# High and low weight tiles as eight separate buffers, the high ones shifted by up to 128 bytes, and four raw buffers in place of five

## The chip, the cores and the metric

The kernel runs on one core of one Trainium2 chip. The metric is the device time of one execution in microseconds (us). Times agree between executions to about 0.1%: the two timed runs of the kernel before gave 1609.97 and 1611.32 us.

## What is computed

The reference is a decoder trunk of two layers over 256 tokens of width 2,048. Each layer normalises x, multiplies it by one wide input projection, sends the columns through a sparse-attention group and a state-space (SSD) group, normalises both results, joins them and multiplies by one output projection, whose result is added to x:

```python
def hybrid_layer(x, ...):
    h = rmsnorm(x, norm_w)
    proj = jnp.einsum("bsd,dp->bsp", h, w_in)          # 2048 -> 11856 columns
    (q, kc, vc, ks, vs, kw, vw, gate, z_attn, xbc, dt, z_ssm) = split_columns(proj)
    ...                                                # attention with three branches, conv, SSD
    mixed = jnp.concatenate([y_attn, y_ssm], axis=-1)  # 4096 wide
    return x + jnp.einsum("bsm,md->bsd", mixed, w_out)
```

All weights arrive in float32. The two projections of the two layers are nearly all of the weight bytes.

## The kernel before

**Weights as high and low parts.** A float32 product is put together from products in a shorter format (F32R). Each weight piece is split in two: `hi` is the weight rounded to F32R, `lo` is the weight less `hi`. The activations are split in the same way. A product is then activation-high times weight-high, activation-low times weight-high, and activation-high times weight-low.

**Slots.** The weights are cut into 250 pieces per layer, 500 in all (`NS` = 250, `DEPTH` = 2). A piece is one tile of 128 partitions by 1,024 float32, 512 KB, and the work on it is called a slot. 186 pieces per layer belong to the input projection (93 column tiles of 128 columns, each in two halves of the 2,048 inputs) and 64 to the output projection.

- In a slot of the input projection (L950 to L968) the weights are the stationary operand and the activations `src[k]` stream: 8 matmuls of `wh[:, k]` with 512 columns (high and low activations side by side) and 8 of `wl[:, k]` with 256 columns, in pairs: two high, two low. In layer 0 the streamed tiles are called `h`, in layer 1 `s`; each is 128 by 512 float32, 2,048 bytes per partition.
- In a slot of the output projection (`block`, L977 to L987) it is the other way: the mixed activations are stationary and the weights stream, 512 columns each. A slot has 12 matmuls, 8 that stream `wh` and 4 that stream `wl`.

**The pipeline of a weight piece.** SP issues the transfer of piece `d` from HBM into a raw tile `wr` (`pump_dma`, L147 to L152). ScalarE copies the raw tile into `wh` (L160, through the helper at L122). VectorE subtracts `wh` from the raw tile into `wl` (L166, through the helper at L125). TensorE reads `wh` and `wl`.

- Each of `wr`, `wh` and `wl` is a tag of the tile pool with a number of buffers used in turn: `NR` = 5 raw, `NH` = 4 high, `NL` = 4 low. A buffer is 4,096 bytes per partition, and the buffers of one tag lie one behind the other. A tile that takes a buffer again waits until the readers of the tile before it in this buffer are done.
- `split(i)` (L154 to L167) is called in slot `i`. It emits the high copy up to piece `i + LH` and the low one up to piece `i + LL` (both 2 ahead), and after each low one it calls `pump_dma`, which emits the transfers up to `state["lo"] + NR`. So the transfer that is emitted behind the low copy of piece `j` is the one of piece `j + 5`. It takes the raw buffer of piece `j`, and waits for that low copy.
- The instructions stand in each engine's queue in the order in which the program emits them; nothing reorders them there.

**Start.** Before the first slot the program issues by hand the first piece (three parts on ScalarE's queue), and on SP's queue the input x in five parts, pieces 1 to 4 between them (`pump_one`, L179), and then the parameters `prm` and the constants `cst` (L202, L203).

**Other work.** Between slots the program runs generators (`sides`) for convolution, SSD, attention and norms, whose instructions are placed by waiting counts written out by hand (`WAITS`). The tile `KT{g}` (L268), which holds the attention keys, has rows of 272 float32: its four parts `kt[:, b, t]` start 1,088 bytes apart.

Of the kernel before, what the change touches and what calls it, by code (L numbers as in the profile page):

```python
# [12 lines left out]
F32R = mybir.dt.float32r  # L13
# [74 lines left out]
def body(ctx: ExitStack, tc: tile.TileContext, wst, w1, xin, xtk, pos, w2, par, con, fin, y):  # L88
# [1 line left out]
    ACT, DVE, PE, POOL = nc.scalar, nc.vector, nc.tensor, nc.gpsimd  # L90
    RS, RA = 5, 1
    FIRST = ((0, 256), (256, 512), (512, 1024))
    NR, NH, NL, LH, LL = 5, 4, 4, 2, 2

    pp = ctx.enter_context(tc.tile_pool(name="pp", bufs=1))
    qq = ctx.enter_context(tc.tile_pool(name="qq", bufs=1, space=bass.MemoryType.PSUM))
# [5 lines left out]
    def sb(shape, tag, dt=F32, bufs=1):  # L102
        cnt[0] += 1
        return pp.tile(shape, dt, tag=tag, name=f"{tag}_{cnt[0]}", bufs=bufs)
# [11 lines left out]
    def act(out, in_, f=AF.Copy, **kw):  # L116
        if f in (AF.Ln, AF.Exp) and table[0] != AF.Exp:
            ACT.preload_act_table_set("natural_log_exp_and_others")
            table[0] = AF.Exp
        elif f in (AF.Silu, AF.Sin):  # L120
            table[0] = f
        ACT.activation(out, in_, f, **kw)  # L122
# [10 lines left out]
    def lo(out, full, hi):  # L133
        tt(out, full, f(hi), OP.subtract)
# [9 lines left out]
    raw, hi_t, lo_t = {}, {}, {}  # L144
    state = {"dma": 0, "hi": 0, "lo": 0}

    def pump_dma():  # L147
        while state["dma"] < min(state["lo"] + NR, DEPTH * NS):
            d = state["dma"]
            raw[d] = sb([128, 1024], "wr", bufs=NR)  # L150
            nc.sync.dma_start(raw[d], wst[d])
            state["dma"] += 1  # L152

    def split(i, part=1024):  # L154
        while state["hi"] < min(i + LH + 1, DEPTH * NS):
            j = state["hi"]
            state["hi"] += 1
            hi_t[j] = sb([128, 1024], "wh", F32R, bufs=NH)
            for c in range(0, 1024, part):
                act(hi_t[j][:, c:c + part], raw[j][:, c:c + part])  # L160
        while state["lo"] < min(i + LL + 1, DEPTH * NS):
            j = state["lo"]
            state["lo"] += 1
            lo_t[j] = sb([128, 1024], "wl", F32R, bufs=NL)
            for c in range(0, 1024, part):
                lo(lo_t[j][:, c:c + part], raw[j][:, c:c + part], hi_t[j][:, c:c + part])  # L166
            pump_dma()  # L167
# [11 lines left out]
    def pump_one():  # L179
        d = state["dma"]  # L180
        raw[d] = sb([128, 1024], "wr", bufs=NR)
        nc.sync.dma_start(raw[d], wst[d])
        state["dma"] += 1

    def load_x(a, b):
        c = NK + SEQ * a if a else 0
        nc.sync.dma_start(xw[:, c:NK + SEQ * b], xin[:, c:NK + SEQ * b])
# [10 lines left out]
    load_x(8, 12)  # L198
    pump_one()
    load_x(12, 16)  # L200
    pump_one()
    nc.sync.dma_start(prm, par[0])  # L202
    nc.sync.dma_start(cst, con)  # L203
    pump_dma()

    ident = cst[:, C_ID:C_ID + 128]
# [166 lines left out]
            scaled(attn[:, k], nw0[:, k:k + 1], h[k])  # L373

    state["hi"] = state["lo"] = 1
    hi_t[0] = sb([128, 1024], "wh", F32R, bufs=NH)
    lo_t[0] = sb([128, 1024], "wl", F32R, bufs=NL)
    for j, (a, b) in enumerate(FIRST):
        make_h((0, 1, 2)[j], (1, 2, 4)[j])
        act(hi_t[0][:, a:b], raw[0][:, a:b])  # L380
        lo(lo_t[0][:, a:b], raw[0][:, a:b], hi_t[0][:, a:b])
    make_h(4, 8)
    split(1 - LH)
    nc.gpsimd.dma_start(posi, bass.AP(tensor=pos.tensor, offset=pos.offset, ap=[[0, 128], [1, SEQ]]))

# [19 lines left out]
    for L in range(DEPTH):  # L405
# [524 lines left out]
        for it in ITEMS:  # L930
            if it[0] == "w":
                kv, j = it[1], it[2]
# [19 lines left out]
            if it[0] == "p":  # L952
# [3 lines left out]
                wh = hi_t[i].rearrange("p (k c) -> p k c", k=8)  # L956
                wl = lo_t[i].rearrange("p (k c) -> p k c", k=8)
                n = 2 if L or slot else 1
                for a in range(0, 8, n):
# [4 lines left out]
                    if L == 0 and slot == 0:  # L964
                        for _ in range(WARM[a]):
                            mm(pz, wz[:, 0:128], wz, True, True)
                flush()
                split(i)  # L968
            else:
                cb, kp, half = it[1:]  # L970
# [53 lines left out]
                if last4:  # L1024
                    if kp == 4:
                        split(i + 1)
                        for kq in range(4, 8):
                            block(kq, 0)
                            if kq == 4:
                                split(i + 1)  # L1030
                        add(0)
                        out_norm(0)
                    block(kp, 1)
                    if kp == 7:
                        add(1)
                        out_norm(1)
                else:
                    block(kp, 0)
                    flush()
                    if kp == 7:  # L1040
                        add(0)
                    block(kp, 1)
                    split(i)
                    if kp == 7:
                        add(1)
                        if half and L + 1 < DEPTH:
                            sides.append(turn())
# [136 lines left out]
```

## Time and profile before

| | us |
|---|---|
| median of the two timed runs | 1610.64 |
| the profiled execution, its own time | 1612.35 |
| span of the profiled execution, first to last instruction | 1610.6 |
| TensorE (PE) busy | 1582.5 |
| VectorE (DVE) busy | 1219.2 |
| ScalarE (ACT) busy | 1056.3 |
| GpSimd (POOL) busy | 383.9 |

The profiled execution took 1.7 us more than the median of the runs, and its span is that median to 0.1 us. How to read the profile: "busy" is the time in which an engine had an instruction under way. Matmuls are pipelined, so their single durations overlap and the spacing of their starts is what one of them costs. PEld is the load of the stationary operand, which runs beside the matmuls. The chain of work is followed back from the last instruction, at each step to what released it.

### The profile page before, as it was taken

Reading aid. Unit: us, or ns where it says so; the run is one execution under the profiler, and the core shown is the slowest. Engines: PE = TensorE matmul, PEld = TensorE weight load, DVE = VectorE, ACT = ScalarE, POOL = GpSimd, SP = SyncE. Lnnn points to the kernel's source line nnn. Section 1 sums busy time; section 2 is a strip of 40 time slices with the busy share of each in tenths; the row PEclk is TensorE's granted clock in tenths of the full one; section 3 lists DMA queues with packets and bytes.
Section 4 is the critical chain, followed back from the end, with each engine's and each line's share of the span. In section 5 each row is a group of like instructions: output and inputs, shape, how many; then the busy total and the mean of one; then the engine's idle time right before and its main releaser. Section 6 shows DMA issues by size and latency. Waiting matters only on the chain.

```text
span 1610.6 us, 24881 instructions
## 1 busy us (share of the span) xinstructions
PE 1582.5 (98%) x9042; PEld 1353.0 (84%) x9042; DVE 1219.2 (76%) x2113; ACT 1056.3 (66%) x1918; POOL 383.9 (24%) x314
## 2 busy tenths in 40 slices
PE   8999999999899999999999999999998999999997
PEld 7888888878788888888888888888787888888876
DVE  6888988887688786674578888888867878766654
ACT  6587777754687787544456777777447778865443
POOL 1233433431123231100012333333301323210010
PEclk9999999999999999999999999999999999999999
DMA  7575566677444444565646666666863454455653
GB/s 267 187 253 189 191 205 209 206 248 256 130 157 134 156 151 153 195 192 166 207 158 197 201 206 192 190 200 222 273 224 121 142 158 145 157 169 171 235 177 110
DMA packets 101994, 301.98 MB, mean 188 GB/s; under 512 B 9952, under 2 KB 26912, under 8 KB 101744
## 3 DMA queue, kind: packets, MB, share of 16 engines
q1 hardware_dynamic: 101024, 297.99, 56.4%
q0 software_dynamic: 416, 1.88, 0.4%
q8 instruction: 71, 1.16, 0.3%
q10 hardware_dynamic: 432, 0.52, 0.1%
q14 instruction: 51, 0.42, 0.1%
HBM read 298.20 MB, written 2.16 MB: 186 GB/s over the span
## 4 chain that ended last, share of the span: by engine, by line
PE 93%; DVE 2%; ACT 2%; DMA 1%; issue 1%; POOL 0%; ACTq 0%; SPq 0%; DVEq 0%; POOLq 0%
PE ppj L137 77%; PE po L137 7%; PE pb L137 6%; DVE wl L125 1%; ACT wh L122 1%; PE pt L137 1%; DMA wr<-wst 1%; PE pt L523 0%; PE pt L766 0%; PE po L773 0%; PE pt L767 0%; DMA V<-w 0%; DVE xT L125 0%; ACT A L122 0%; DVE A L128 0%
## 5 line engine op out<-in xcount | busy, mean ns | idle before, releaser
L125 DVE TENSOR_TENSOR wl<-wr,wh 128x1024 fp32r<-128x1024 f32 (+1 forms) x502 | 642.6, 1285 | 218.4 <-ACT wh L122 217.5
L122 ACT ACTIVATE wh<-wr 128x1024 fp32r<-128x1024 f32 (+1 forms) x502 | 517.8, 1048 | 85.6 <-PE ppj L137 46.2
L137 PE MATMUL ppj<-h,wh 128*128 128x512 f32 x1456 | 464.6, 400 | 3.1 <-DVE h L128 3.1
L137 PE MATMUL ppj<-s,wh 128*128 128x512 f32 x1456 | 462.7, 399 | 0.0
L137 PEld LDWEIGHTS ppj<-h,wl 128*128 128x128 f32 x1456 | 274.9, 189 | 65.1
L137 PEld LDWEIGHTS ppj<-s,wl 128*128 128x128 f32 x1456 | 274.4, 188 | 65.1
L137 PE MATMUL ppj<-h,wl 128*128 128x256 f32 x1456 | 288.3, 279 | 0.0
L137 PE MATMUL ppj<-s,wl 128*128 128x256 f32 x1456 | 287.3, 279 | 0.0
L340 POOL TENSOR_TENSOR uu<-uu,rr 128x256 f32<-128x256 f32 x120 | 147.7, 1232 | 525.3 <-DVE uu L125 524.0
L137 PEld LDWEIGHTS ppj<-h,wh 128*128 128x128 f32 x1456 | 223.4, 190 | 9.5 <-issue 3.3
L137 PEld LDWEIGHTS ppj<-s,wh 128*128 128x128 f32 x1456 | 222.8, 189 | 5.0 <-issue 2.7
L122 ACT ACTIVATE ev<-ppj 128x256 f32<-128x256 f32 x182 | 68.7, 378 | 210.7 <-PE ppj L137 193.7
L137 PE MATMUL ppj<-wh,h 128*128 128x512 f32 x384 | 120.4, 391 | 0.0
L137 PE MATMUL ppj<-wh,s 128*128 128x512 f32 x384 | 120.1, 391 | 0.0
L340 POOL TENSOR_TENSOR za<-za,rr 128x256 f32<-128x256 f32 x34 | 39.6, 1165 | 274.6 <-DVE za L125 239.2
L137 PEld LDWEIGHTS ppj<-wh,h 128*128 128x128 f32 x384 | 72.1, 188 | 15.6 <-DVE xT L125 0.7
L137 PEld LDWEIGHTS ppj<-wh,s 128*128 128x128 f32 x384 | 72.1, 188 | 15.5 <-DVE xT L125 0.7
L125 DVE TENSOR_TENSOR uu<-ppj,ev 128x256 f32<-128x256 f32 x116 | 48.7, 420 | 47.1 <-ACT ev L122 46.9
L122 ACT ACTIVATE A<-A,nm 128x128 f32<-128x128 f32 (+2 forms) x192 | 75.4, 394 | 7.8 <-DVE nm L716 7.6
L137 PE MATMUL ppj<-wl,s 128*128 128x512 f32 x192 | 74.9, 390 | 0.8 <-DVE wl L125 0.8
L137 PE MATMUL ppj<-wl,h 128*128 128x512 f32 x192 | 74.8, 389 | 0.0
L128 DVE SCALAR_TENSOR_TENSOR att<-uu,par,att 128x255 f32<-128x255 f32 (+2 forms) x96 | 60.5, 630 | 2.3
(244 smaller groups left out, 1980.9 us busy)
## 6 DMA issues: line engine op xcount, KB each, us to landing
wr<-wst SPq DMA_DIRECT2D x499, 512.0 KB, 3.5
V<-w SPq DMA_DIRECT2D x64, 256.0 KB, 4.8
B<-cum SPq DMA_DIRECT2D x16, 512.0 KB, 4.6
B<-cum SPq DMA_DIRECT2D x16, 256.0 KB, 5.7
xT<-xtk SPq DMA_DIRECT2D x4, 512.0 KB, 6.8
att<-xin SPq DMA_DIRECT2D x3, 512.0 KB, 8.5
att<-fin POOLq DMA_DIRECT2D x1, 1024.0 KB, 8.9
y<-xT SPq DMA_DIRECT2D x2, 512.0 KB, 2.7
```

The lines of the kernel that those rows point to most:

```text
L122: ACT.activation(out, in_, f, **kw)
L125: DVE.tensor_tensor(out, a, b, op=op)
L128: DVE.scalar_tensor_tensor(out, a, s, b, op0=op0, op1=op1)
L137: PE.matmul(out, lhsT, rhs, start=start, stop=stop, skip_group_check=True)
L340: POOL.tensor_tensor(dst, dst, rr[0], op=OP.mult)
```

## The change

- The four high buffers become four tags of one buffer each, `wh0` to `wh3`, each 32 float32 wider (1,056). Piece `j` uses tag `j % 4`, and of it the 1,024 elements from `SHIFT[j % 4]` on: 0, 8, 16 or 32 elements, which is 0, 32, 64 or 128 bytes.
- The four low buffers become four tags of one buffer each, `wl0` to `wl3`, of the old size and unshifted. Since a tag gets its place when it is first used, the eight tiles now lie between other tiles.
- There are four raw buffers in place of five, and one `pump_one` at the start goes with the fifth.

```diff
-    NR, NH, NL, LH, LL = 5, 4, 4, 2, 2
+    NR, NH, LH, LL = 4, 4, 2, 2
+    SHIFT = (0, 8, 16, 32)
...
+    def high(j):
+        t = sb([128, 1024 + 32], f"wh{j % NH}", F32R)
+        return t[:, SHIFT[j % NH]:SHIFT[j % NH] + 1024]
+
     def pump_dma():
         while state["dma"] < min(state["lo"] + NR, DEPTH * NS):
...
-            hi_t[j] = sb([128, 1024], "wh", F32R, bufs=NH)
+            hi_t[j] = high(j)
...
-            lo_t[j] = sb([128, 1024], "wl", F32R, bufs=NL)
+            lo_t[j] = sb([128, 1024], f"wl{j % NH}", F32R)
...
     load_x(12, 16)
-    pump_one()
     nc.sync.dma_start(prm, par[0])
...
-    hi_t[0] = sb([128, 1024], "wh", F32R, bufs=NH)
-    lo_t[0] = sb([128, 1024], "wl", F32R, bufs=NL)
+    hi_t[0] = high(0)
+    lo_t[0] = sb([128, 1024], "wl0", F32R)
```

## Rows read from the trace of the kernel before

**Rows 1.** The page: span, busy time of the engines, clock, chain that ended last.

```profile
span 1610.6 us, 24881 instructions
PE 1582.5 (98%) x9042; PEld 1353.0 (84%) x9042; DVE 1219.2 (76%) x2113; ACT 1056.3 (66%) x1918; POOL 383.9 (24%) x314
...
PEclk9999999999999999999999999999999999999999
...
PE 93%; DVE 2%; ACT 2%; DMA 1%; issue 1%; POOL 0%; ACTq 0%; SPq 0%; DVEq 0%; POOLq 0%
```

**Rows 2.** TensorE's waits in its loads: engine, waiter, releaser: us in total, times, longest.

```profile
PEld ppj L137 <- ACT wh L122: 4.7, 17, 1.7
...
PEld po L137 <- DVE wl L125: 2.7, 3, 1.3
...
PEld ppj L137 <- DVE wl L125: 1.2, 1, 1.2
```

**Rows 3.** Timeline of TensorE, input projection, layers 0 and 1: start, us, instruction, count.

```profile
311.17 0.63 PE L137 MATMUL ppj<-h,wh 128*128 128x512 f32 x2
...
316.75 0.62 PE L137 MATMUL ppj<-h,wh 128*128 128x512 f32 x2
...
900.22 0.62 PE L137 MATMUL ppj<-s,wh 128*128 128x512 f32 x2
...
902.31 0.63 PE L137 MATMUL ppj<-s,wh 128*128 128x512 f32 x2
```

**Rows 4.** Timeline of TensorE, output projection of layer 0.

```profile
766.98 0.62 PE L137 MATMUL ppj<-wh,h 128*128 128x512 f32 x2
...
771.75 0.61 PE L137 MATMUL ppj<-wh,h 128*128 128x512 f32 x2
```

**Rows 5.** Timeline of TensorE, attention scores of layer 0.

```profile
470.24 1.27 PE L137 MATMUL pb<-KT,Q 128*128 128x272 f32 x9
471.35 0.62 PE L137 MATMUL ppj<-h,wh 128*128 128x512 f32 x2
```

**Rows 6.** Groups by shape: count, busy us, mean ns; idle before.

```profile
L125 DVE TENSOR_TENSOR wl<-wr,wh 128x1024 fp32r<-128x1024 f32 x499 | 641.1, 1290 | 215.3 <-ACT wh L122 214.4
...
L137 PEld LDWEIGHTS ppj<-h,wh 128*128 128x128 f32 x1456 | 223.4, 190 | 9.5 <-issue 3.3 <-ACT wh L122 2.9 <-DVE h L128 2.8
...
L128 DVE SCALAR_TENSOR_TENSOR A<-uu,par,A 128x253 f32<-128x253 f32 x32 | 15.4, 483 | 1.1
...
L128 DVE SCALAR_TENSOR_TENSOR att<-att,par,uu 128x256 f32<-128x256 f32 x32 | 15.4, 480 | 0.0
```

**Rows 7.** All instructions on the raw tiles: waits on transfers, and time to landing.

```profile
  DMA wr<-wst: 2.9, 1
...
DMA to landing us min/median/max: 3.1/3.5/10.7
```

**Rows 8.** Timeline of ScalarE: two copies of a piece into its high tile.

```profile
773.53 1.06 ACT L122 ACTIVATE wh<-wr 128x1024 fp32r<-128x1024 f32 x1 [1.66 <-PE ppj L137]
...
1587.64 1.06 ACT L122 ACTIVATE wh<-wr 128x1024 fp32r<-128x1024 f32 x1 [1.59 <-PE pb L137]
```

**Rows 9.** Timeline: the raw copy with the least room, its neighbour's transfer, its first matmul.

```profile
1502.49 1.06 ACT L122 ACTIVATE wh<-wr 128x1024 fp32r<-128x1024 f32 x1 [1.35 <-issue]
...
1495.42 0.33 SPq L151 DMA_DIRECT2D wr<-wst  x1
...
1510.40 0.39 PE L137 MATMUL ppj<-wh,s 128*128 128x512 f32 x1
```

**Rows 10.** Transfers issued from 1495.3 to 1495.6 us and from 11.4 to 12 us: us to landing.

```profile
wr<-wst SPq DMA_DIRECT2D x1, 512.0 KB, 8.5
...
wr<-wst SPq DMA_DIRECT2D x1, 512.0 KB, 8.2
```

**Rows 11.** Timeline at the start: SP's transfers behind x, and ScalarE's copy of piece 4.

```profile
11.46 4.54 SPq L151 DMA_DIRECT2D wr<-wst  x3
...
20.15 1.04 ACT L122 ACTIVATE wh<-wr 128x1024 fp32r<-128x1024 f32 x1
```

## The prediction

> **What bounds the kernel now.** I read the page first: TensorE is busy for 98% of the span, and the chain that ended last lies on it for 93%; the granted clock is full in every slice, which is the 2.4 GHz level [rows 1]. So the time is what the matmuls cost, one start after the other, and an edit pays only if it changes the spacing of the matmuls or a wait of TensorE. Then the waits: all of those on a weight tile come to 4.7 + 2.7 + 1.2 = 8.6 us [rows 2]. A better supply of weights can return no more than that.
>
> The timeline shows the spacing. The edit touches where weights lie, so I take the fixed part of a matmul, its spacing less its columns at one per cycle of 2.4 GHz, and compare operands that lie differently.
>
> - Input projection, layer 0: from 311.17 to 316.75 us there are 8 groups of two high (512 columns) and two low (256), 32 matmuls in 5.58 us, 174.4 ns each; the columns are 1,536 / 4 / 2.4 = 160.0 ns. Fixed part: 14.4 ns [rows 3].
> - Layer 1: 12 matmuls from 900.22 to 902.31 us, 174.2 ns each, so 14.2 ns [rows 3].
> - Output projection, where the weights stream: 21 matmuls of 512 columns from 766.98 to 771.75 us, 227.1 ns each; less 213.3, 13.8 ns [rows 4].
> - Attention scores: 9 matmuls from 470.24 to 471.35 us, 6 of 272 and 3 of 256 columns, 2,400 in all or 1.00 us; 1.11 us less that, over 9, is 12.2 ns [rows 5].
>
> In the program's own list of addresses `h` starts at the same place modulo 2,048 as `wh`, and `s` 256 bytes further; the fixed part doesn't tell them apart. The parts of `KT` start 1,088 bytes apart, so every second one is off by 64 modulo 128, and the list has it 32 bytes off the `Q` tile it is multiplied with. These matmuls are the cheapest of the four. If the place of one operand disturbed the reading of the other, one of these groups would be dearer by it, and none is.
>
> **The change part by part.**
>
> *Places and shifts.* No instruction is added, removed or reshaped. 372 slots have 8 matmuls each with `wh` and 128 slots have 8, 4,000 in all; three of four buffers are shifted, 3,000 matmuls. If the shifts brought them to the cheapest row they would gain 14.2 - 12.2 = 2.0 ns each, 6.0 us. If they took away the whole fixed part, the far end, 3,000 x 14.2 = 43 us. On the other side nothing in rows 3 to 5 is dearer for lying askew; the far end is a load that no longer hides. A load takes 190 ns [rows 6], and the one that follows a low matmul has that matmul's spacing of some 0.23 / 2 = 115 ns; the 75 ns that stick out, in half the 2,976 high loads of the input projection and three buffers of four (1,116), would be 84 us. I take zero: the traced rows lie 2.2 ns apart over operands 0, 32, 64 and 256 bytes askew, and zero is where layers 0 and 1 meet.
>
> The Trainium skill, TensorE: Matmul & The Clock Gate, Back-to-back issue gap, gives an isolated warm matmul N / 2.4 + 2.5 ns. This trace doesn't agree, with 12.2 to 14.4 in place of 2.5; by the page some 11 ns on each matmul would have another cause, and if that were how the tiles lie there would be more to win than my sum has. The same section says that in a stream of loads and matmuls the spacing is set by both, which fits a fixed part that doesn't move with the address.
>
> *VectorE and ScalarE.* The low subtraction reads a shifted tile and the high copy writes one. A subtraction averages 1,290 ns [rows 6]. The trace has an operation on views shifted by 12 bytes: 483 ns for 253 elements, against 480 for 256 unshifted [rows 6]. So a shift costs at most 3 + 3 ns (the three missing elements are some 3 ns); on 375 subtractions that is 2.3 us of an engine that is idle for 24% of the span [rows 1]. Cost on the path: zero; without that cover, 2.3 us.
>
> *Eight tags of one buffer.* A piece still takes the place of the one four before it and waits for the same readers. Cost zero; were the distance shorter by one, the 8.6 us of [rows 2] would be the first to grow.
>
> *Four raw buffers.* The transfer emitted behind the low subtraction of piece j is now that of piece j + 4 and not j + 5. It takes the buffer of piece j in both, waits for the same subtraction and stands at the same place in SP's queue, so what is queued behind it (the transfers of `V` and `B`) sees the same wait. The stream keeps its times and moves by one piece: piece j now lands when piece j + 1 landed before. I matched all issues, landings and copies of the trace. The transfers take 3.5 us in the median and 10.7 at most [rows 7], and past the start nine high copies begin before the landing of the next piece, the first at 773.53 and the last at 1587.64 us [rows 8]. The worst starts at 1502.49; its neighbour was issued at 1495.42 us and took 8.5 us, to 1503.9 [rows 9, 10]. So this copy comes 1.4 us later; the other eight 0.02 to 0.8, 4.2 us in all. Late next are the subtraction and the square of the norm behind it on ScalarE. But the worst copy is first read at 1510.40 us [rows 9], 6.8 us after its old end of 1503.55; the others have 2.9 us or more up to their first matmul, subtraction included. Cost zero; with that cover gone, 4.2 us.
>
> *Start.* Piece 4 no longer goes ahead of `prm` and `cst`. It is issued behind the first low subtraction, at 11.46 us, as the transfer that stood there was, which took 8.2 us behind a longer backlog [rows 10, 11]: at the latest 19.7 us, before its copy at 20.15 [rows 11]. `prm` and `cst` come earlier by one transfer. TensorE waits for x there, whose transfers keep their order. Zero.
>
> **Sum.** 1610.6 (span) + 0 + 0 + 0 + 0 + 0 = 1610.6 us; the profiled execution's own time was 1612.35, 1.7 us above the median of the runs, 1610.64. The forecast for the median is 1610.6 us. Its own range is -6.0 (all shifted matmuls as cheap as the scores) and +4.2 (every late copy on the path), 1604.6 to 1614.8, and about a microsecond on each side for the runs' own spread.
>
> **Rivals.**
>
> - *The fixed part is a clash of the two operands* (faster). For: 14.2 ns against the scores' 12.2. Against: layers 0 and 1, 256 bytes apart, agree to 0.2 ns, and the scores still have 12.2 ns. Time: if the shifted matmuls lose it wholly, 1610.6 - 43 = 1568 us. It decides, for 2% (32 us), from 11 ns per shifted matmul, three quarters of the fixed part.
> - *A shifted weight tile loads more slowly* (slower). Place: the high load that follows a low matmul. For: that load has the least room, 115 ns for 190. Against: the matmuls with `KT` are no dearer for places 32 and 64 bytes off. It decides at 32 / 1,116 = 29 ns more per such load; at the far end, 1610.6 + 84 = 1695 us.
> - *The raw tiles come too late* (within 2%). For: nine copies begin before the landing that now counts. Against: each has 2.9 us or more of room at TensorE. Time: 1614.8 us. ScalarE waits for a raw transfer once in the whole trace, 2.9 us at the start [rows 7].
> - *The change does nothing to the rates but the supply of weights smooths out.* At most 8.6 us: 1602 us. No step leads there.
>
> The Trainium skill, SBUF — State Buffer, Who interferes with whom, says that TensorE has a read port each for the moving operand and for the load and never waits on another engine. By it the first rival's gain is nil; rows 3 and 4 agree in that the spacing holds through the tile positions.
>
> **Chances.** The forecast 0.84; the clash 0.06, half of it beyond 11 ns; the slow load 0.05, of which 0.03 beyond 29 ns; raw tiles on the path 0.03; smoother supply 0.02. What a measurement of this kernel can tell from no change is about 2%, 32 us. So faster 0.03, within 2% 0.94, slower 0.03. The range 1603.0 to 1617.0 takes in the two bounds and the runs' spread, and leaves out the clash, the slow load and the smoother supply where they pass 8 us, some 0.13.
>
> **What would show it.** Right: the same spacing per group of four (0.697 us) and per output matmul (0.227 us) in slots of all four buffers; loads at 190 ns; low subtractions near 1,290 ns; at 1502.5 us a copy that waits for its transfer, and no such wait on TensorE. Wrong: a spacing that differs between slots by the shift of their buffer; new waits of TensorE on `wh` or `wl` beyond 8.6 us; a start in which the copy of piece 4 waits for its transfer and a matmul for it.

## The result, and the profile after

The changed kernel takes 1621.45 us in the median of two runs (1621.41 and 1621.48), against 1610.64 before: a ratio of 1.0063, interval 1.0039 to 1.0088. It is slower by 0.7%, 10.8 us. That is within the 2% that the prediction gave nearly all its chance, and 4.5 us above the range.

The page of the changed kernel, cut to the rows that answer to [rows 1]: span, busy time, granted clock, chain.

```profile
span 1619.6 us, 24873 instructions
...
PE 1591.3 (98%) x9042; PEld 1357.5 (84%) x9042; DVE 1216.5 (75%) x2113; ACT 1056.9 (65%) x1918; POOL 385.5 (24%) x314
...
PEclk9999999999999999999999999999999999999999
...
PE 93%; DVE 2%; ACT 2%; issue 1%; DMA 1%; POOL 0%; ACTq 0%; SPq 0%; DVEq 0%; POOLq 0%
```

The span grew by 9.0 us and TensorE's busy time by 8.8. The clock is the same, the chain is the same, and the other engines are no busier. So TensorE does not wait more; its matmuls cost more. Its waits on the weight tiles, to be read against [rows 2]:

```profile
PEld ppj L138 <- ACT wh L123: 4.6, 17, 1.6
...
PEld po L138 <- DVE wl L126: 2.4, 2, 1.2
...
PEld ppj L138 <- DVE wl L126: 1.2, 1, 1.2
```

They come to 8.2 us, where [rows 2] had 8.6. All instructions on the raw tiles, to be read against [rows 7]: waits on their transfers in us and their number, and the time to landing.

```profile
  DMA wr<-wst: 12.2, 6
...
DMA to landing us min/median/max: 3.1/3.6/9.3
```

ScalarE now waits for a raw transfer six times, 12.2 us in all, and TensorE's waits show none of it. The groups by shape that answer to the first two lines of [rows 6]: count, busy us, mean ns, idle before.

```profile
L126 DVE TENSOR_TENSOR wl<-wr,wh 128x1024 fp32r<-128x1024 f32 x499 | 638.4, 1284 | 223.0 <-ACT wh L123 220.1 <-DMA V<-w 2.1 <-issue 0.2
...
L138 PEld LDWEIGHTS ppj<-h,wh 128*128 128x128 f32 x1456 | 224.7, 190 | 10.4 <-DVE h L129 3.8 <-ACT wh L123 3.2 <-issue 2.8
```

The subtraction did not suffer from the shift (1,284 ns, before 1,290), and the load of a high tile takes 190 ns as before. What did change is the spacing. TensorE's timeline in layer 1, three input slots of high buffers 0, 1 and 2 one behind the other (answers to [rows 3]):

```profile
989.16 0.62 PE L138 MATMUL ppj<-s,wh 128*128 128x512 f32 x2
...
991.96 0.63 PE L138 MATMUL ppj<-s,wh 128*128 128x512 f32 x2
...
994.77 0.63 PE L138 MATMUL ppj<-s,wh 128*128 128x512 f32 x2
...
997.58 0.64 PE L138 MATMUL ppj<-s,wh 128*128 128x512 f32 x2
```

48 matmuls in 8.42 us are 175.4 ns each, where [rows 3] had 174.2. And the output projection of layer 0 (answers to [rows 4]):

```profile
769.94 0.64 PE L138 MATMUL ppj<-wh,h 128*128 128x512 f32 x2
...
777.57 0.63 PE L138 MATMUL ppj<-wh,h 128*128 128x512 f32 x2
```

33 matmuls in 7.63 us are 231.2 ns each, where [rows 4] had 227.1. The fixed part over the 213.3 ns of 512 columns went from 13.8 to 17.9 ns.

Nothing happens at one place. A slot starts 1.3 us later than before at slot 150, 4.3 at slot 250, 6.2 at slot 400 and 9.0 at the last. Inside the slots, with the starts of their matmuls taken from the trace, the loss is this (medians over the slots of a layer, from the start of a slot's first matmul to that of its last, in ns):

| high buffer, its shift | 0, 0 B | 1, 32 B | 2, 64 B | 3, 128 B |
|---|---|---|---|---|
| input slot, layer 1, before | 2687 | 2674 | 2674 | 2674 |
| input slot, layer 1, after | 2683 | 2698 | 2683 | 2683 |
| output slot, layers 0 and 1, before | 2494, 2494 | 2494, 2494 | 2494, 2494 | 2494, 2493 |
| output slot, layers 0 and 1, after | 2525, 2523 | 2552, 2550 | 2574, 2560 | 2550, 2531 |

Summed over all slots, gap by gap and without gaps over 300 ns, in which TensorE waits, the input slots lost 3.9 us and the output slots 4.9: 8.8 of the 9.0 us of the span. One number speaks against the shift as the cause: buffer 0 is not shifted, and its output slots are longer by 29 to 31 ns too.

### The profile page after: what moved, and what is told of

It reads as the page before. It is cut to its first block, busy times and chain, and to the rows that moved or that the text cites. A ratio compares the mean times of both kernels' runs of the same rounds, so it can differ in the third digit from the quotient of the medians.

```text
span 1619.6 us, 24873 instructions
## 1 busy us (share of the span) xinstructions
PE 1591.3 (98%) x9042; PEld 1357.5 (84%) x9042; DVE 1216.5 (75%) x2113; ACT 1056.9 (65%) x1918; POOL 385.5 (24%) x314
## 4 chain that ended last, share of the span: by engine, by line
PE 93%; DVE 2%; ACT 2%; issue 1%; DMA 1%; POOL 0%; ACTq 0%; SPq 0%; DVEq 0%; POOLq 0%
PE ppj L138 77%; PE po L138 7%; PE pb L138 6%; DVE wl L126 1%; ACT wh L123 1%; PE pt L138 1%; DMA wr<-wst 1%; PE pt L527 0%; PE pt L770 0%; PE pt L771 0%; PE po L777 0%; DVE xT L126 0%; DMA V<-w 0%; ACT A L123 0%; DVE A L129 0%
## 5 line engine op out<-in xcount | busy, mean ns | idle before, releaser
L138 PE MATMUL ppj<-h,wl 128*128 128x256 f32 x1456 | 291.8, 281 | 0.0
```

Of the source, the lines that this page charges most:

```text
L138: PE.matmul(out, lhsT, rhs, start=start, stop=stop, skip_group_check=True)
```

## The experiments

Two things moved in the program's own list of addresses. By the place of a tile I mean its first byte in that list modulo 256. The shift moves a high tile against its own buffer. The padding of 128 bytes moves everything that lies behind it. Before, all tiles that TensorE reads in a projection start at the same place modulo 256 bytes (`wh`, `wl` and `h` at the same place modulo 2,048, `s` 256 further). After, `wl0` and the first `h` lie 128 bytes off `wh0`, `wh1` with its shift lies 160 bytes off `wl1`, and so on. My theory was that the place of TensorE's operands relative to each other sets the spacing; the rivals were the raw buffers, the separate tags, the shift alone, the absolute place, and disturbance by other engines.

**Taking the change apart.** Four kernels, each with four raw buffers.

Four raw buffers alone:

```diff
-    NR, NH, NL, LH, LL = 5, 4, 4, 2, 2
+    NR, NH, NL, LH, LL = 4, 4, 4, 2, 2
...
-    pump_one()
```

> The kernel before with four raw buffers and one early transfer less; weight tiles as before. The changed kernel lost 10.8 us, spread over all slots, with no new wait of TensorE. Theory places (the spacing of the matmuls follows from where their operands lie): 1610.6, within 1 us of before, and the 11 gaps of an output slot sum to 2494 ns as before. Rival raw (the raw buffer that is gone sets the loss): about 1621.

Eight tags as well, neither shifted nor padded (against the changed kernel):

```diff
-    SHIFT = (0, 8, 16, 32)
+    SHIFT = (0, 0, 0, 0)
...
-        t = sb([128, 1024 + 32], f"wh{j % NH}", F32R)
+        t = sb([128, 1024], f"wh{j % NH}", F32R)
```

> The changed kernel without shifts and without the 128 bytes of padding: eight tiles of 4,096 bytes, interleaved with the activation tiles as in the changed kernel, four raw buffers. All tiles that TensorE reads in projections again start at the same place modulo 512 (the s tiles 256 bytes off). Theory places modulo some hundred bytes: 1610.6. Rival separate tags (the large distances, or the waits that go with tags of one buffer): about 1621.

Padding, but no shift (against the changed kernel):

```diff
-    SHIFT = (0, 8, 16, 32)
+    SHIFT = (0, 0, 0, 0)
```

> The changed kernel with all four shifts 0 but the 128 bytes of padding left, so only the distances between the tiles are those of the changed kernel. Theory distances (tiles 128, 256 or 384 bytes askew of each other are what costs): 1621, output slots at 2520 to 2575 ns. Theory shift (what costs is where the high tile starts, 32, 64 or 128 bytes further): 1610.6, output slots at 2494. If both take part: between, some 1614 to 1618.

Shift and padding, but two tags, so that the tiles lie together (against the changed kernel):

```diff
-        t = sb([128, 1024 + 32], f"wh{j % NH}", F32R)
+        t = sb([128, 1024 + 32], "wh", F32R, bufs=NH)
...
-            lo_t[j] = sb([128, 1024], f"wl{j % NH}", F32R)
+            lo_t[j] = sb([128, 1024], "wl", F32R, bufs=NH)
```

> Shifts and padding as in the changed kernel, but the four high tiles lie one behind the other, and so do the four low ones, as before. The shifted places modulo 512 against the low tiles and the activations are others than in the changed kernel: the high pieces lie 192, 32, 0 and 0 (piece j % 4 = 0, 3, 2, 1 by address) bytes differently. Theory shift: 1619 to 1622. Theory distances: slower than before, by an amount that may differ from 10.8 us by a few us. Rival interleaving of the tags alone: 1610.6.

Measured, with 1611.14 us before in the same runs: four raw buffers 1612.64 us (ratio 1.0009, 1.0000 to 1.0018); eight tags 1612.64 (1.0006, 0.9997 to 1.0015); padding without shift 1622.06 (1.0070, 1.0056 to 1.0083); shift and padding together 1620.86 (1.0061, 1.0049 to 1.0074). The raw buffers and the tags cost 1.5 us in the medians, at most 2.9 by the interval, and nothing that these runs tell from zero; two later runs with four raw buffers and all places equal (all tiles moved, and multiples of 256 bytes, below) have ratios of 1.0000 and 0.9999. The padding alone brings the whole loss. Its output slots in layer 0, none of whose tiles is shifted:

```profile
770.21 0.63 PE L138 MATMUL ppj<-wh,h 128*128 128x512 f32 x2
...
777.13 0.63 PE L138 MATMUL ppj<-wh,h 128*128 128x512 f32 x2
```

30 matmuls in 6.92 us, 230.7 ns each. In the run with the tiles together, buffer 0 has its high tile, its low tile and both sets of activations at one place modulo 256, and its output slots are back at 2493 and 2494 ns (medians of the layers), while those of the other buffers stand at 2530 to 2563. So it is neither the shift as such nor the distance in kilobytes.

Buffer 3 seems to speak against this: there its padding and its shift add up to 256 bytes, so all its tiles are at one place too, and yet its output slots take 2530 ns. The single spacings explain it. One such slot, behind a slot of buffer 2:

```profile
665.70 0.39 PE L138 MATMUL ppj<-wl,s 128*128 128x512 f32 x1
...
667.08 0.39 PE L138 MATMUL ppj<-wl,s 128*128 128x512 f32 x1
...
667.76 0.39 PE L138 MATMUL ppj<-wl,s 128*128 128x512 f32 x1
```

Six matmuls from 665.70 to 667.08 us are 230 ns each, and the three behind them 226.7, as before. In the medians over its 32 output slots the first seven spacings are 225 to 241 ns and the last four 227; in 26 of the 32 all of the last four are back there. So what a slot at other places leaves behind is carried over into the next one and mostly settles within some eight matmuls. The changed kernel's buffer 3, whose tiles are at one place as well, behaves alike (medians of 228 to 232, then 227; 18 of 32 slots are back).

**One tile at a time.** Next I moved tiles by 128 bytes with an unused tile in front of them. All tiles (an unused tile ahead of `wh`):

```diff
+    sb([128, 32], "pa")
     hi_t[0] = sb([128, 1024], "wh", F32R, bufs=NH)
```

> Four raw buffers, weight tiles as before, and 128 bytes of unused memory ahead of them: all of wh, wl, h and s lie 128 bytes further, and their distances are those of before. Theory relative place: 1611 to 1612, output slots at 2494 ns. Theory absolute place: slower, towards 1620.

Only the low tiles:

```diff
     hi_t[0] = sb([128, 1024], "wh", F32R, bufs=NH)
+    sb([128, 32], "pa")
     lo_t[0] = sb([128, 1024], "wl", F32R, bufs=NL)
+    sb([128, 96], "pb")
```

> Four raw buffers, and only the four low tiles lie 128 bytes further; the activations lie 512 further, at the same place modulo 512 as the high tiles. Theory relative place: slower, 1615 to 1620, with the gaps around the low matmuls longer (input slots at about 2685 to 2700, output slots at 2510 to 2550 ns). Rival only the high tile counts: 1611 to 1612.

Only the high tiles:

```diff
+    sb([128, 32], "pa")
     hi_t[0] = sb([128, 1024], "wh", F32R, bufs=NH)
+    sb([128, 96], "pb")
     lo_t[0] = sb([128, 1024], "wl", F32R, bufs=NL)
```

> Four raw buffers, and only the four high tiles lie 128 bytes further modulo 512 (low tiles and activations 512 further, at the place of before modulo 512). Theory relative place: slower, 1615 to 1622. Rival only the low tile counts: 1611 to 1612. Beside the run with only the low tiles moved it says whether the loss of the changed kernel is the sum of both.

With 1611.82 us before: all moved 1611.97 (ratio 1.0000, 0.9991 to 1.0009), low alone 1621.34 (1.0063, 1.0048 to 1.0079), high alone 1624.87 (1.0081, 1.0064 to 1.0098). Both tiles count, and only against each other and the activations; the two single moves cost more than I expected. They cost it in different slots: with the low tiles moved, input slots stand at 2681 to 2687 ns (medians), about as long as expected, and output slots at 2569 to 2570, longer than expected; with the high ones moved, at 2710 and at 2518 to 2519. The output slots of the run with the low tiles moved:

```profile
767.37 0.62 PE L137 MATMUL ppj<-wh,h 128*128 128x512 f32 x2
...
777.17 0.63 PE L137 MATMUL ppj<-wh,h 128*128 128x512 f32 x2
```

42 matmuls in 9.80 us, 233.3 ns each. The run with the high tiles moved, input slots first and then output slots:

```profile
316.26 0.64 PE L137 MATMUL ppj<-h,wh 128*128 128x512 f32 x2
...
319.79 0.40 PE L137 MATMUL ppj<-h,wh 128*128 128x512 f32 x1
...
771.37 0.62 PE L137 MATMUL ppj<-wh,h 128*128 128x512 f32 x2
...
777.55 0.62 PE L137 MATMUL ppj<-wh,h 128*128 128x512 f32 x2
```

20 matmuls in 3.53 us are 176.5 ns each in the input slots, and 27 in 6.18 us are 228.9 in the output slots.

**TensorE alone.** All tiles are parts of one tile here, so that each place is exact:

```python
mm(ps, at(WH, dh, 128 * k, 128), at(H, dx, 512 * k, 512), ...)           # input order: high, 512 columns
mm(ps[:, 0:256], at(WL, dl, 128 * k, 128), at(H, dx, 512 * k, 256), ...)  # low, 256 columns
```

> The kernel's work is left out: one tile is filled, and TensorE alone runs 17 sections of 48 matmuls in the order of an input slot (three slots; high tile, low tile and activations at places set by three numbers in bytes), then 17 sections of 36 matmuls in the order of an output slot, then 6 and 5 such sections beside the high copies and low subtractions of three pieces. The output is one of zeros and a few sums. Theory own operands (TensorE's own two reads disturb each other when their tiles don't start at the same place modulo 256 bytes): with nothing else running, the section at 0, 0, 0 takes 8.36 us (48 x 174.2 ns), the one with all three 128 bytes further the same, and one with 128 bytes in the high or low tile alone some 0.3 to 1% more. Theory absolute place: the section with all three moved is dearer too. Rival other engines (the reads are disturbed by the copies and subtractions of ScalarE and VectorE): all sections that run alone take the same to 0.1%, and only those beside copies differ.

TensorE's timeline, one row for each section. The names: p is the order of an input slot and o of an output slot; then the bytes by which the high tile lies further, l and those of the low tile, and a or b for activations 0 or 128 bytes further; _x beside copies and subtractions. The last number is the count of matmuls.

```profile
43.84 8.64 PE L120 MATMUL p128l0a<-op 128*128 128x512 f32 x48
...
52.31 8.56 PE L120 MATMUL p0l128a<-op 128*128 128x512 f32 x48
...
69.10 8.52 PE L120 MATMUL p128l128b<-op 128*128 128x512 f32 x48
...
85.88 8.72 PE L120 MATMUL p64l0a<-op 128*128 128x512 f32 x48
...
111.16 8.45 PE L120 MATMUL p192l192a<-op 128*128 128x512 f32 x48
...
136.15 8.53 PE L120 MATMUL p256l256a<-op 128*128 128x512 f32 x48
...
169.90 8.35 PE L120 MATMUL o0l0a<-op 128*128 128x512 f32 x36
...
194.69 8.55 PE L120 MATMUL o0l128a<-op 128*128 128x512 f32 x36
...
277.74 8.32 PE L120 MATMUL o256l256a<-op 128*128 128x512 f32 x36
...
294.29 8.67 PE L120 MATMUL o4l0a<-op 128*128 128x512 f32 x36
...
327.88 8.63 PE L120 MATMUL p128l0a_x<-op 128*128 128x512 f32 x48
```

With nothing else running the places move a section by up to 4% (8.32 to 8.67 us). The starts of the single matmuls give, for four of an input slot: 696.5 ns with all three moved by 128 bytes, 696.8 at 256/256, 699.5 at 0/128, 706.0 at 128/0, 712.9 at 64/0 and 690.3 at 192/192 (high/low against the activations). For one of an output slot: 227.1 ns at 0/0, 226.7 at 256/256, 233.2 at 0/128, 228.9 at 128/0, 236.4 at 4/0. Copies and subtractions beside it change nothing (706.0 and 705.5 ns). The rival of other engines falls, the absolute place falls, and 256 bytes count as nothing. The section at 0, 0, 0 has no row of its own, since it follows the first matmuls of the run under the same name; the one with all three moved stands for it, with 174.1 ns a matmul or 8.36 us for 48; the last 48 starts under that name give the same, 696.6 ns for four. The effect was larger than the 0.3 to 1% that I expected: 1.4% at 128/0 and 2.4% at 64/0, with 0.4% at 0/128 inside. The output numbers 233.2 and 228.9 are those of the kernel with low and with high tiles moved, 233.3 and 228.9.

**The table of places.** The same, with every place in steps of 32 bytes.

> The kernel's work is left out, as in the probe before: TensorE alone runs 64 sections of 48 matmuls in the order of an input slot and 64 of 36 in the order of an output slot, with the high tile and the low tile each 0, 32, ... 224 bytes off the activations. In the probe before, four matmuls of an input slot took 696 ns at 0/0, 690 at 192/192, 693 at 64/64, 706 at 128/0, 713 at 64/0; one of an output slot 227.1 ns at 0/0 and 228 to 236 at other places. Theory relative place: these come back to 1 ns, the rest of the table lies between 690 and 715 for four and between 226.5 and 237 ns for one, and 0/0 is the best or nearly the best for output slots but not for input slots. Rival drift (what differs is when a section runs, not its place): repeated places differ from the first probe by as much as places differ from each other.

```profile
161.28 8.70 PE L117 MATMUL p64l0a<-op 128*128 128x512 f32 x48
...
178.30 8.49 PE L117 MATMUL p64l64a<-op 128*128 128x512 f32 x48
...
481.22 8.47 PE L117 MATMUL p192l192a<-op 128*128 128x512 f32 x48
...
565.31 8.34 PE L117 MATMUL o0l0a<-op 128*128 128x512 f32 x36
...
957.29 8.60 PE L117 MATMUL o160l224a<-op 128*128 128x512 f32 x36
```

Places that both probes hold agree to 0.6 ns in output slots. In input slots they agree to 2.5 ns for four matmuls (192/192: 692.4 here, 690.3 there) but for one, 0/64, with 706.6 here and 700.2 there; the theory said 1 ns. It does not drift: in either probe this section holds its own value from its fourth group of four to its last. What differs, besides the chip that it ran on, is the section before it, 0/32 here and 64/0 there. So the same places can run at two spacings, and which of them seems to hang on what came before; that was not tested by itself. Places differ by up to 21 (713.3 at 128/32). In output slots 0/0 is the best of all 64, 227.3 ns, and the rest lie from 228.8 to 234.4. In input slots nine places are below the 696.5 ns of equal places, 192/192 the lowest.

With this table the loss of a kernel can be worked out from its program: for each slot the places of its two weight tiles against its activation tiles from the program's list of addresses, the table's number less that at 0/0, times the matmuls. The kernels here had been run before the table was.

| kernel | by the table, us: input + output slots | measured inside the slots, us | median less that of before, us |
|---|---|---|---|
| the changed kernel | 6.0 + 6.4 | 3.9 + 4.9 | 10.8 |
| padding, no shift | 10.5 + 5.8 | 5.6 + 4.6 | 10.9 |
| shift, tiles together | 8.0 + 4.4 | 5.2 + 4.3 | 9.7 |
| low tiles 128 B off | 6.2 + 9.1 | 2.9 + 7.1 | 9.5 |
| high tiles 128 B off | 13.1 + 2.5 | 11.2 + 2.5 | 13.1 |
| all 128 B off | 0 | -1.2 + 0.0 | 0.2 |

The order of the parts comes out right but for the two smallest of the input slots, and the medians are 62 to 87% of the table's sums. Some of the difference is the last spacing of each slot, which the third column leaves out. The table's sections hold one set of places for three slots; in the kernels the places change from slot to slot, and what is carried over counts. An input slot of the padded kernel at 128/0, behind one at 0/128, four groups of four:

```profile
980.51 0.64 PE L138 MATMUL ppj<-s,wh 128*128 128x512 f32 x2
...
981.22 0.62 PE L138 MATMUL ppj<-s,wh 128*128 128x512 f32 x2
...
981.91 0.63 PE L138 MATMUL ppj<-s,wh 128*128 128x512 f32 x2
...
982.61 0.64 PE L138 MATMUL ppj<-s,wh 128*128 128x512 f32 x2
```

The groups take 714, 693 and 700 ns by the exact starts, and the slot 2697. In the kernel with the high tiles moved, where every slot is at 128/0, each group takes 706 to 707 and the slot 2710. That is some of what the padded kernel's input slots lose less than the table says; the rest is open.

**Back to the best places.** The changed kernel with every number made a multiple of 256 bytes:

```diff
-    SHIFT = (0, 8, 16, 32)
+    SHIFT = (0, 64, 0, 64)
...
-        t = sb([128, 1024 + 32], f"wh{j % NH}", F32R)
+        t = sb([128, 1024 + 64], f"wh{j % NH}", F32R)
```

> The changed kernel (eight separate tiles at different distances, shifted high tiles, four raw buffers) with every number made a multiple of 256 bytes: padding 256, shifts 0, 256, 0, 256. The tiles lie 0, 256, 512 and so on off each other. Theory relative place modulo 256: 1611 to 1612.5, output slots at 2494 ns. Rival modulo more than 256 (or shifts as such): about 1621.

And the kernel with four raw buffers, with weights 192 bytes (48 elements) off in input slots alone:

```diff
+PLACE = 48
...
+    def place(j, tag):
+        t = sb([128, 1024 + 64], tag, F32R, bufs=NH)
+        o = PLACE if WITEMS[j % NS][0] == "p" else 0
+        return t[:, o:o + 1024]
...
-            hi_t[j] = sb([128, 1024], "wh", F32R, bufs=NH)
+            hi_t[j] = place(j, "wh")
...
-            lo_t[j] = sb([128, 1024], "wl", F32R, bufs=NL)
+            lo_t[j] = place(j, "wl")
...
-    hi_t[0] = sb([128, 1024], "wh", F32R, bufs=NH)
-    lo_t[0] = sb([128, 1024], "wl", F32R, bufs=NL)
+    hi_t[0] = place(0, "wh")
+    lo_t[0] = place(0, "wl")
```

> Four raw buffers, weight tiles one behind the other and 256 bytes wider; high and low weights lie 192 bytes off the activations modulo 256 in the pieces of the input projection, and 0 off in those of the output projection. In the table of places four matmuls of an input slot took 692 ns at 192/192 (690 in the first probe) against 696 at 0/0. Theory relative place modulo 256: an input slot gets 16 to 24 ns shorter, 372 of them 6 to 9 us, so 1602 to 1606 us and faster than the kernel before by 0.3 to 0.6%; output slots stay at 2494 ns. Rival the place of before is the best there is beside the other engines: 1611 to 1620.

With 1611.71 us before, the first takes 1611.71 us (ratio 0.9999, 0.9990 to 1.0008): eight separate shifted tiles at uneven distances, and no loss. Its output slots:

```profile
766.26 0.61 PE L138 MATMUL ppj<-wh,h 128*128 128x512 f32 x2
...
777.14 0.61 PE L138 MATMUL ppj<-wh,h 128*128 128x512 f32 x2
```

48 matmuls in 10.88 us, 226.7 ns each. The second takes 1603.48 us (0.9949, 0.9936 to 0.9963), 0.5% faster than the kernel before and 1.1% faster than the changed one. Its page, span and busy time:

```profile
span 1604.6 us, 24873 instructions
...
PE 1576.3 (98%) x9042; PEld 1352.7 (84%) x9042; DVE 1216.6 (76%) x2113; ACT 1055.7 (66%) x1918; POOL 387.9 (24%) x314
```

And TensorE's timeline in its input slots of layer 0:

```profile
311.07 0.62 PE L138 MATMUL ppj<-h,wh 128*128 128x512 f32 x2
...
317.97 0.62 PE L138 MATMUL ppj<-h,wh 128*128 128x512 f32 x2
```

40 matmuls in 6.90 us are 172.5 ns each, against 174.4 before [rows 3]. An input slot went from 2674 to 2646 ns, a little more than expected. By the table it is 372 x 4 x (692.4 - 696.5) = -6.1 us, by the first probe's 690.3 it is -9.2; the median moved by -8.2.

**Can a spacing be put together from single pairs?**

> The kernel's work is left out: TensorE alone runs 112 sections of 48 matmuls in the order of an input slot, in which every second activation tile lies 32, 64, ... 224 bytes further than the others, with the high and the low tile 0, 64, 128 or 192 bytes off. Theory one pair (a spacing follows from the tile that streams and the tile that is loaded meanwhile, and not from the rest): some of these places are cheaper for all four matmuls together than the best of the first table (690 to 692 ns), down to 678 where all four take their shortest single spacings seen (226, 226, 113, 113). Rival sequence (the four spacings are coupled, what one gains another gives back): none is under 690 by more than 2 ns.

```profile
169.66 8.43 PE L116 MATMUL p0l64c<-op 128*128 128x512 f32 x48
...
924.42 8.71 PE L116 MATMUL p128l192h<-op 128*128 128x512 f32 x48
```

The best of 112 is 689.1 ns for four, with single spacings of 230, 226, 116 and 118, and the worst 712.0. Where one of the four reached its shortest, another was longer. So my theory of single pairs fell here and the rival held: the places act on the whole sequence, and a table of pairs cannot be added up.

## Why the prediction was wrong

*What bounds the kernel* held: the time is what the matmuls cost one after the other, and the loss is a change of their spacing that no other engine shows.

*Places and shifts* is the step that failed. It put at zero a term that measures +9.0 us in the span (3.9 inside the input slots, 4.9 inside the output slots) and +10.8 in the medians. It also counted the wrong matmuls: the 3,000 with a shifted high tile. The padding moves what lies behind it, low tiles and activations too, and without any shift it costs the same, 10.9 us. Its readings of the rows were wrong in this.

- "The fixed part doesn't tell them apart", said of `h` and `s`: they lie 256 bytes from each other, and the probe has 696.5 ns for places that are equal and 696.8 for 256/256. The one distance that the two layers offered is one that costs nothing. In the kernel before every operand of the projections lay at the same place modulo 256, so its trace had no row of the case that the change makes. For the same reason [rows 3] and [rows 4] do not show that the spacing holds "through the tile positions".
- "These matmuls are the cheapest of the four", said of `KT` and `Q`, the only rows with operands askew (32 to 224 bytes modulo 256 in the list): these have 272 and 256 columns, and their 12.2 ns had nothing of the same form at equal places to stand against. In the probe, one form in 64 places ranges over 21 ns for four. A row of another shape bounds nothing here, and the bound "nothing is dearer for lying askew" rested on it.

The range's lower end of -6.0 came from the same rows, and its upper end of +4.2 from the late copies alone: it held nothing for dearer matmuls. The loss of 10.8 us lies inside the far ends of -43 and +84 that the step named, and the range of 1603.0 to 1617.0 then cut it off by giving the two rivals about 1 in 10. That the result is within 2% says nothing for the step: no cost of some ten microseconds could have left that band.

*The clash of the two operands* was the right mechanism for a rival, read in one direction alone. I asked what shifting would take away from a clash that is there, and not what it would add where there is the least. Both happen: 192/192 takes 4 to 6 ns from four matmuls, 64/0 adds 15 to 16.

*A shifted weight tile loads more slowly* had the right sign and the wrong thing in it: loads stay at 190 ns, the loss comes without any shift, and tiles shifted by 256 bytes lose nothing.

*The sentence on ports*, by which TensorE's moving operand and load have a read port each, put the gain of the first rival at nil. The Trainium skill, SBUF — State Buffer, Who interferes with whom, calls the two ports independent and says that TensorE waits on no other engine. The second half agrees with the runs here: copies beside the matmuls changed nothing (706.0 and 705.5 ns). By the first half the place of one operand against the other would not matter; the measurement differs, with 690 to 713 ns for the same four matmuls and TensorE alone at work, and it decides.

*Eight tags, VectorE and ScalarE, the start* held: eight tags 1612.64 us, the same as four raw buffers without them, subtractions of 1,284 ns, and no slot at the start that is later.

*Four raw buffers* held, in its mechanism too. In the run with four raw buffers alone, where no spacing has changed, nine copies wait for their transfer: the one at the start that waited before, and eight of the nine that the step counted, from the one at 773.53 to the one at 1587.64 us by the times of before. All instructions on the raw tiles, waits on their transfers:

```profile
  DMA wr<-wst: 19.0, 9
```

These 19.0 us are not all delay: ahead of the same nine copies ScalarE was idle for 13.9 us in the kernel before, for the start's transfer (2.9) and for other reasons, so some 5 us are new, where 4.2 were worked out. TensorE's waits on the weight tiles are 8.2 us there, and the time is not told from that of before (ratio 1.0009, 1.0000 to 1.0018).

## What to carry to other kernels

When TensorE is the bound, and in a stream like this one (F32R, a load of 128 by 128 for each matmul), the start of the weight tile against the start of the activation tile, modulo 256 bytes, is a parameter of the kernel like any other: a padding of 128 bytes on a tile moved everything behind it and cost 0.7%. Padding and shifts in multiples of 256 bytes leave it alone, and a probe of 48 matmuls for each place finds a better one in a single run; it was worth 0.5% here. And a trace in which all operands lie alike says nothing of operands that lie otherwise: an effect that the rows cannot show is unknown, not zero.

## What the runs showed of the hardware

- With TensorE alone at work, its spacing depends on where the two tiles that it reads, one streamed and one loaded, lie relative to each other modulo 256 bytes: 690 to 713 ns for four matmuls of an input slot (two of 512 and two of 256 columns), 226.7 to 236.4 ns for one of 512 columns with the weights streaming. Moving both by the same 128 bytes changes nothing (696.6 and 696.5 ns), and neither do 256 bytes between them (696.8).
- Four bytes can be enough: with the high tile 4 bytes off, an output matmul takes 236.4 ns, the longest seen, while four matmuls in the input order take 697.5 ns, 1 more than at equal places.
- Equal places are not the best for every sequence: 192/192 beats 0/0 in the input order (690 to 692 against 696.5), and 0/0 is the best of 64 in the output order.
- What ran before counts too: behind a slot at other places, most output slots at equal places need some eight matmuls to come back to 227 ns and some do not within their twelve, and one pair of places, 0/64, held 700 ns for four in one probe and 707 in the other.
- Why the places act is not shown by these runs; that the spacing follows the two places together, and not either alone, is.
